# New cost numbers for an order of work that is laid out ahead, and later loads of the memory rows, in an encoder layer

## The chip, the cores and the metric

The kernel runs on one core of a Trainium2 chip. The metric is the device time of one execution in microseconds (us). Three runs of the kernel before gave a median of 1152.73 us (1152.61 to 1153.55). Five engines are spoken of: TensorE (PE in the profile; its weight loads are PEld), VectorE (DVE), ScalarE (ACT), GpSimd (POOL) and SyncE (SP), which issues most of the loads.

## The reference

One encoder layer for a sequence of 256 tokens of width 2048, in float32. Cut to what matters:

```python
# h = rms_norm(x); one combined input projection
x = x + W_out @ concat(mla(h), diff_attention(h))    # 8 MLA heads, 4 difference heads
x = x + cross_attention(rms_norm(x), rms_norm(mem))  # 4 heads into 256 memory tokens
x = x + swiglu(rms_norm(x))                          # hidden width 5632
return rms_norm(x)

def rms_norm(x, g, eps=1e-6):
    return x * rsqrt(mean(x * x, axis=-1) + eps) * g
```

The MLA half projects the normed rows to a query latent of 512, a key and value latent of 256 and a rotary key of 64, norms the latents and projects them up; rotary tables (sine and cosine of position times frequency) are computed from the positions. The memory has 256 rows of 2048.

## The kernel before

Weights are streamed from memory once. Each weight tile (wraw, up to 1 MB) is split into a high part wh, a cast on ScalarE, and a low part wl, the remainder, a subtraction on VectorE. Activations are split in the same way (names ending in _h and _l). A product is then three matmuls: high by high, high by low, low by high (mm in the listing). The rows on which a wide product rests are handled in pairs of k-tiles. A plain pair takes the three matmuls for each quarter of the result. A pair of kind W takes seven products of sums in place of eight ones, so it needs sums and forms of the activations (sums, forms_h, forms_l) and of the weights (tsum) from VectorE and ScalarE. The string DN_KINDS says which pairs of the down projection are of which kind.

The stages, in time order by the profile: the latent product (6 to 48 us: 16 k-tiles of x0T against w_in_lat, 512 columns into acc and 320 into acckv), the wide input projection and the MLA heads (from 48 us), the difference heads, the output product (wide_add over w_out), the product of the memory with w_xk, the cross-attention, and from about 470 us on the feed-forward layer, whose hidden chunks alternate with groups of the down projection (wide_add over w_dn). In the list called groups each entry gives the chunks computed before it and the order in which its pairs are then taken.

Nothing of this is issued in the order of the code. Each call on an engine is recorded by Plan.record as an Op with three modelled numbers from Plan.cost: how long the engine is busy, how long until the result is usable (lag), and how long a transfer takes. Plan.emit makes a list schedule: first one run that takes operations as they come ready, then two rounds in which each operation has a wanted time, found backwards from the modelled starts of TensorE's work. In Plan.run every engine has a time at which it is free, transfers share one queue, and of the operations that could start soon the one wanted first is taken. The order that comes out is the program order of each engine. Real waits are semaphores, put in for data and for buffers that are handed on; so a wrong number in the model never makes a wrong result, only an order in which an engine stands behind something that is late. op.after(other, False) adds a rule for the order alone and puts in no semaphore. All recorded operations carry the line of record's inner function, L224, so the profile is read by tile names.

Four parts of the code are spoken of.

- Squares of the memory rows. The rows (tiles mn, four of 512 KB from in_mem, buffers of the pool act, which has 24) are loaded by GpSimd and squared with a running sum by ScalarE (junk<-mn, eight operations, sums in mss); VectorE adds them up and GpSimd takes the power (rstdm), and VectorE scales the product with w_xk by it (xk). rstdm is not needed before that.
- The first k-tile. Its weight tile is loaded and cast in two pieces of 512 and 320 columns (cut=QL); VectorE makes x0T_h from xraw and gains.
- The rope tables. GpSimd computes them (ang, a1r, turns, prod) from posi, which SP loads behind the first seven k-tiles. Its queue also holds the powers rstd (for the norm of x), rq and rkv (for the latents). VectorE's cq<-acc,rstd and ckv<-acckv,rstd scale the latents; TensorE transposes them (pt<-ident,ckv).
- The group changes of the down projection. res are the sums of a finished hidden chunk; TensorE transposes them (pt<-ident,res), ScalarE copies them back and makes hT_h, VectorE makes hT_l; W pairs use forms_h and forms_l of the same data.

Of the kernel before, what the change touches and what calls it, by code (L numbers as in the profile page):

```python
# [18 lines left out]
P = 128  # L19
# [159 lines left out]
class Plan:  # L179


    HANDOVER, CHOICE = 0.06, 0.3

    def __init__(self, tc):
# [31 lines left out]
    def record(self, engine, method, args, kw):  # L216
        out = [x for x in (kw.get("out", args[0] if args else None), kw.get("accum_out")) if isinstance(x, Ref)]
        ins = [x for x in list(args) + list(kw.values()) if isinstance(x, Ref) and not any(x is o for o in out)]
        busy, lag, transfer = self.cost(engine, method, out, ins, kw, args)

# [8 lines left out]
        for ref, writes in [(r, True) for r in out] + [(r, False) for r in ins]:  # L229
            t, mask = ref.tile, ref.mask()  # L230
# [12 lines left out]

    def cost(self, engine, method, out, ins, kw, args):
        if method == "dma_start":
            size = max(x.cols() for x in out + ins) * 512
            return 0.86 if engine == "gpsimd" else 0.06, 2.0 + size / 375e3, size / 381e3
        n = max([x.cols() for x in out[:1]] + ([x.cols() for x in ins[:1]] if "reduce" in method else []))
        if engine == "tensor":
            if method == "transpose":  # L250
                return 0.108, 0.33, 0.0
            return 0.0134 + n / 2400, 0.2134 + n / 2400, 0.0
        if engine == "gpsimd":
            t = 0.15 + n * 0.0045
            return t, t + 0.1, 0.0
        if engine == "vector":
            if n <= 16 and "reduce" not in method:
                t = 0.07
            elif method == "scalar_tensor_tensor":
                t = 0.127 + n * 1.05e-3  # L260
            elif method in ("tensor_scalar", "memset"):
                t = 0.03 + n / 1024
            else:
                t = 0.068 + n / 960
            return t, t + 0.082, 0.0
        t = 0.044 + 0.855e-3 * n if ins and ins[0].tile.whole else 0.092 + 0.842e-3 * n
        if isinstance(kw.get("scale"), Ref):
            t += 0.09
        if kw.get("accum_out") is not None:
            t += 0.093  # L270
        return t, t + (0.2 if kw.get("accum_out") is not None else 0.1), 0.0

# [8 lines left out]
    def run(self, chain, wanted, emit):  # L281
# [11 lines left out]
        for engine in ("sync", "scalar"):  # L293
            in_turn([o for o in self.ops if o.engine == engine and o.transfer])
        open_ops, free, queue, picks, starts, ended = {}, {}, 0.0, {}, {}, 0.0
        emitted, to_go, slots = [], {}, {}
# [24 lines left out]
        for _ in self.order:  # L321
# [20 lines left out]
            if o.transfer:  # L342
                begun = max(start, queue)
                queue, end = begun + o.transfer, begun + o.lag
            starts[o] = start
# [93 lines left out]
def encoder_block(tc: tile.TileContext, a, out):  # L439
# [736 lines left out]
    for tt in range(NT):  # L1176
        n = nat("xk")
# [279 lines left out]
```

## Time and profile before

| what | value |
|---|---|
| median of three runs | 1152.73 us (1152.61 to 1153.55) |
| the profiled execution | 1153.09 us |
| its span in the trace | 1151.2 us |
| TensorE busy | 1132.5 us, 98% of the span |
| VectorE busy | 1017.4 us, 88% |
| ScalarE busy | 695.4 us, 60% |
| GpSimd busy | 54.8 us, 5% |
| read from memory | 219.11 MB |

The span is from the first to the last instruction that the trace shows; 1.9 us of the execution lie outside. Busy time of TensorE is read from pipelined matmuls: one of 512 columns shows 0.39 us, but the next one starts about 0.23 us after it. A number in brackets behind a row of the timeline is the idle time of that engine before the instruction, and what ended it. In tables by stage, the columns are the stretch, its length, and the busy time and number of instructions of each engine, TensorE's granted clock, the share of the DMA engines' time and the rate in GB/s.

### The profile page before, as it was taken

Reading aid. Unit: us, or ns where it says so; the run is one execution under the profiler, and the core shown is the slowest. Engines: PE = TensorE matmul, PEld = TensorE weight load, DVE = VectorE, ACT = ScalarE, POOL = GpSimd, SP = SyncE. Lnnn points to the kernel's source line nnn. Section 1 sums busy time; section 2 is a strip of 40 time slices with the busy share of each in tenths; the row PEclk is TensorE's granted clock in tenths of the full one; section 3 lists DMA queues with packets and bytes.
Section 4 is the critical chain, followed back from the end, with each engine's and each line's share of the span. In section 5 each row is a group of like instructions: output and inputs, shape, how many; then the busy total and the mean of one; then the engine's idle time right before and its main releaser. Section 6 shows DMA issues by size and latency. Waiting matters only on the chain.

```text
span 1151.2 us, 14663 instructions
## 1 busy us (share of the span) xinstructions
PE 1132.5 (98%) x5360; PEld 941.0 (82%) x5360; DVE 1017.4 (88%) x1378; ACT 695.4 (60%) x999; POOL 54.8 (5%) x75
## 2 busy tenths in 40 slices
PE   8999999999999999999999999999999999999997
PEld 6889888888888788887878888888788888888786
DVE  4788768778988767799999999999999999999995
ACT  6757445466765545656665565666665565756762
POOL 4920000000000000000000000000000000000000
PEclk9999999999999999999999999999999999999999
DMA  9734354456554444555545556565455565556453
GB/s 353 292 135 170 110 183 145 150 180 228 193 209 179 147 178 158 184 179 198 213 172 216 210 194 216 183 219 200 169 217 212 190 219 183 201 208 250 153 200 122
DMA packets 35496, 222.16 MB, mean 193 GB/s; under 512 B 4320, under 2 KB 5600, under 8 KB 11104
## 3 DMA queue, kind: packets, MB, share of 16 engines
q1 hardware_dynamic: 33696, 216.60, 52.6%
q0 software_dynamic: 864, 3.15, 0.8%
q10 hardware_dynamic: 864, 1.47, 0.4%
q8 instruction: 42, 0.69, 0.2%
q14 instruction: 30, 0.25, 0.1%
HBM read 219.11 MB, written 2.10 MB: 192 GB/s over the span
## 4 chain that ended last, share of the span: by engine, by line
PE 81%; DVE 10%; POOL 4%; ACT 2%; issue 2%; DMA 1%; SPq 0%; POOLq 0%; DVEq 0%; ACTq 0%
PE acc L224 63%; PE q L224 13%; DVE wl L224 3%; PE pt L224 2%; POOL prod L224 1%; DVE res L224 1%; PE qT L224 1%; DMA wraw<-in_w_in_lat 1%; POOL ang L224 1%; DVE tsum L224 1%; POOL turns L224 1%; DVE nm L224 1%; PE psc L224 1%; DVE sums L224 1%; DVE forms_l L224 1%
## 5 line engine op out<-in xcount | busy, mean ns | idle before, releaser
L224 DVE TENSOR_TENSOR wl<-wraw,wh 128x1024 fp32r<-128x1024 f32 (+2 forms) x401 | 449.2, 1133 | 92.2 <-ACT wh L224 90.7
L224 ACT CAST wh<-wraw 128x1024 fp32r<-128x1024 f32 (+2 forms) x401 | 388.0, 978 | 234.7 <-PE acc L224 192.3
L224 ACT CAST wh<-tsum 128x1024 fp32r<-128x1024 f32 (+1 forms) x118 | 119.5, 1017 | 127.4 <-DVE tsum L224 73.7
L224 DVE TENSOR_TENSOR wl<-tsum,wh 128x1024 fp32r<-128x1024 f32 (+1 forms) x118 | 137.9, 1174 | 5.8 <-PE acc L224 4.0
L224 PE MATMUL acc<-wh,x2n_h 128*128 128x512 f32 x320 | 124.7, 390 | 0.0
L224 PE MATMUL acc<-wh,x2n_l 128*128 128x512 f32 x320 | 124.6, 389 | 0.0
L224 PE MATMUL q<-wh,forms_h 128*128 128x512 f32 x231 | 91.4, 396 | 1.4 <-ACT res L224 1.4
L224 PE MATMUL q<-wh,forms_l 128*128 128x512 f32 x231 | 90.0, 390 | 0.0
L224 PE MATMUL acc<-wl,x0T_h 128*128 128x512 f32 x224 | 89.2, 398 | 0.6 <-DVE wl L224 0.6
L224 PE MATMUL acc<-wh,x0T_h 128*128 128x512 f32 x224 | 89.0, 397 | 0.6 <-DVE x0T_h L224 0.6
L224 PE MATMUL acc<-wh,x0T_l 128*128 128x512 f32 x224 | 88.6, 395 | 0.0
L224 PE MATMUL acc<-wl,x2n_h 128*128 128x512 f32 x320 | 86.1, 390 | 0.0
L224 PE MATMUL q<-wl,forms_h 128*128 128x512 f32 x231 | 81.0, 392 | 1.1 <-DVE wl L224 1.1
L224 DVE TENSOR_TENSOR tsum<-tsum,wraw 128x512 f32<-128x512 f32 x118 | 80.7, 684 | 0.8
L224 PE MATMUL acc<-wh,forms_l 128*128 128x512 f32 x192 | 74.9, 390 | 0.0
L224 PE MATMUL acc<-wh,forms_h 128*128 128x512 f32 x192 | 74.9, 390 | 0.0
L224 DVE TENSOR_TENSOR tsum<-wraw 128x1024 f32<-128x1024 f32 (+1 forms) x64 | 72.2, 1134 | 1.5 <-DMA wraw<-in_w_out 1.5
L224 PE MATMUL acc<-wh,hT_h 128*128 128x512 f32 x188 | 73.4, 390 | 0.0
L224 PE MATMUL acc<-wh,hT_l 128*128 128x512 f32 x188 | 73.2, 389 | 0.0
L224 PE MATMUL acc<-wl,forms_h 128*128 128x512 f32 x192 | 72.9, 390 | 0.0
L224 PEld LDWEIGHTS acc<-wh,x2n_l 128*128 128x128 f32 x320 | 60.1, 188 | 12.5
L224 PEld LDWEIGHTS acc<-wh,x2n_h 128*128 128x128 f32 x320 | 60.1, 188 | 12.5
(377 smaller groups left out, 2149.7 us busy)
## 6 DMA issues: line engine op xcount, KB each, us to landing
wraw<-in_w_gate SPq DMA_DIRECT2D x44, 1024.0 KB, 4.8
wraw<-in_w_up SPq DMA_DIRECT2D x44, 1024.0 KB, 4.8
wraw<-in_w_dn SPq DMA_DIRECT2D x41, 1024.0 KB, 4.8
wraw<-in_w_in SPq DMA_DIRECT2D x24, 1024.0 KB, 4.8
wraw<-in_w_out SPq DMA_DIRECT2D x16, 1024.0 KB, 4.9
wraw<-in_w_in_lat SPq DMA_DIRECT2D x5, 832.0 KB, 6.2
wraw<-in_w_xk SPq DMA_DIRECT2D x4, 1024.0 KB, 5.5
wraw<-in_w_xq SPq DMA_DIRECT2D x4, 1024.0 KB, 4.8
```

Source lines behind the costliest of these rows:

```text
L224: getattr(getattr(self.tc.nc, engine), method)(*[made(x) for x in args], **{k: made(x) for k, x in kw.items()})
```

## The change

It has three parts.

- Costs. Plan.cost gets other numbers: issuing a load takes 0.55 us on GpSimd and 0.45 us on SP and ScalarE (before 0.86 and 0.06); arithmetic on GpSimd takes 0.59, 0.7 or 1.0 us by its columns (before 0.15 + 0.0045 for each); VectorE's scalings are priced by whether they read PSUM; an activation with a bias tile costs as one with a scale tile; lags of TensorE and ScalarE are shorter. Plan.run starts each engine at a time of its own (BEGUN), lets small transfers pass the queue, and adds 0.9 us to loads started in the first 5 us.
- Memory rows. Each of their four loads is placed in the order after the last weight split of the output product (load.after(mixed, False)). This is a rule of the order; no semaphore is added.
- Groups two and three of the down projection take pair 4 before pair 2.

```diff
+    BEGUN = {"tensor": 0.6, "vector": 0.8, "scalar": 0.7, "sync": 0.7, "gpsimd": 0.3}
...
         if method == "dma_start":
             size = max(x.cols() for x in out + ins) * 512
-            return 0.86 if engine == "gpsimd" else 0.06, 2.0 + size / 375e3, size / 381e3
+            return {"gpsimd": 0.55, "sync": 0.45, "scalar": 0.45}[engine], 2.0 + size / 375e3, size / 381e3
         n = max([x.cols() for x in out[:1]] + ([x.cols() for x in ins[:1]] if "reduce" in method else []))
+        in_psum = bool(ins) and ins[0].tile.whole
         if engine == "tensor":
-            if method == "transpose":
-                return 0.108, 0.33, 0.0
-            return 0.0134 + n / 2400, 0.2134 + n / 2400, 0.0
+            t = 0.108 if method == "transpose" else 0.0134 + n / 2400
+            return t, t + 0.14, 0.0
         if engine == "gpsimd":
-            t = 0.15 + n * 0.0045
-            return t, t + 0.1, 0.0
+            if method in ("memset", "affine_select", "tensor_copy"):
+                t = 0.1 + n * 1.2e-3
+            else:
+                t = 0.59 if n == 1 else 0.7 if n == 2 else 1.0
+            return t, t + 0.03, 0.0
         if engine == "vector":
             if n <= 16 and "reduce" not in method:
-                t = 0.07
+                t = 0.08
             elif method == "scalar_tensor_tensor":
                 t = 0.127 + n * 1.05e-3
-            elif method in ("tensor_scalar", "memset"):
-                t = 0.03 + n / 1024
+            elif method == "tensor_scalar":
+                t = 0.129 + n * 1.035e-3 if in_psum else n / 960
+            elif method == "tensor_tensor_reduce":
+                t = 0.145 + n / 960
+            elif method == "tensor_copy":
+                t = n / 960
             else:
                 t = 0.068 + n / 960
             return t, t + 0.082, 0.0
-        t = 0.044 + 0.855e-3 * n if ins and ins[0].tile.whole else 0.092 + 0.842e-3 * n
-        if isinstance(kw.get("scale"), Ref):
-            t += 0.09
+        t = 0.044 + 0.855e-3 * n if in_psum else 0.092 + 0.842e-3 * n
+        if isinstance(kw.get("scale"), Ref) or isinstance(kw.get("bias"), Ref):
+            t += 0.09 if n < 512 else 0.15
         if kw.get("accum_out") is not None:
             t += 0.093
-        return t, t + (0.2 if kw.get("accum_out") is not None else 0.1), 0.0
+        return t, t + (0.15 if kw.get("accum_out") is not None else 0.08), 0.0
...
-        open_ops, free, queue, picks, starts, ended = {}, {}, 0.0, {}, {}, 0.0
+        open_ops, free, queue, picks, starts, ended = {}, dict(self.BEGUN), 0.0, {}, {}, 0.0
...
             if o.transfer:
-                begun = max(start, queue)
-                queue, end = begun + o.transfer, begun + o.lag
+                begun = max(start, queue) if o.transfer > 0.15 else start
+                queue, end = max(queue, begun + o.transfer), begun + o.lag + (0.9 if start < 5.0 else 0.0)
...
+    mixed = last_split[0]
...
-            nc.gpsimd.dma_start(out=mn, in_=a["mem"][tt * P:(tt + 1) * P, c * 1024:(c + 1) * 1024])
+            load = nc.gpsimd.dma_start(out=mn, in_=a["mem"][tt * P:(tt + 1) * P, c * 1024:(c + 1) * 1024])
+            load.after(mixed, False)
...
-    groups = [([0], (0, 1, 4, 2, 5, 3)), ([1, 2], (0, 1, 2, 4, 5, 3, 7, 6)), ([3, 4], (0, 1, 2, 4, 5, 3, 7, 6))]
+    groups = [([0], (0, 1, 4, 2, 5, 3)), ([1, 2], (0, 1, 4, 2, 5, 3, 7, 6)), ([3, 4], (0, 1, 4, 2, 5, 3, 7, 6))]
```

SP's loads keep their order. Three places show how the others move. The recorded line is L224 before and L225 after.

**ScalarE, the first k-tiles.** Before, behind its two loads of the first weight tile:

```order
L224 CAST wh<-wraw 128x512
L224 ACTIVATE junk,mss<-mn 128x512
L224 CAST wh<-wraw 128x320
L224 ACTIVATE x0T_h<-xraw,gains 128x256
L224 ACTIVATE junk,mss<-mn 128x512
```

After:

```order
L225 CAST wh<-wraw 128x512
L225 CAST wh<-wraw 128x320
L225 ACTIVATE x0T_h<-xraw,gains 128x256
L225 CAST wh<-wraw 128x512
L225 CAST wh<-wraw 128x320
```

The squares of the memory rows left this place (six more stood a little later in it); all eight now stand among the casts of the product with w_xk. On GpSimd the four loads of mn went from the head of the queue to behind the four powers rd of the difference heads, ahead of x1Tr and rstdm.

**VectorE, end of the latent product.** The splits of 1024 columns are of the first weights of the wide input projection, which follows. Before:

```order
L224 TENSOR_TENSOR wl<-wraw,wh 128x1024 x6
L224 TENSOR_SCALAR cq<-acc,rstd_539 128x512 x2
L224 TENSOR_SCALAR ckv<-acckv,rstd_539 128x320
L224 TENSOR_SCALAR rq<-ss 128x1
L224 TENSOR_SCALAR ckv<-acckv,rstd_539 128x320
```

After:

```order
L225 TENSOR_TENSOR wl<-wraw,wh 128x1024 x4
L225 TENSOR_SCALAR cq<-acc,rstd_496 128x512 x2
L225 TENSOR_TENSOR wl<-wraw,wh 128x1024
L225 TENSOR_SCALAR ckv<-acckv,rstd_496 128x320
L225 TENSOR_SCALAR rq<-ss 128x1 x2
L225 TENSOR_SCALAR ckv<-acckv,rstd_496 128x320
```

The scalings of the latents, which need GpSimd's rstd, moved ahead of the fifth and the sixth of those splits.

**VectorE, the first changed group of the down projection.** Here res_7258 (after: res_7259) and res_7287 are the newly finished hidden chunk, of which hT is made, and res_6561 and res_6585 the one of which forms are made. Before:

```order
L224 TENSOR_TENSOR forms_l<-res_6561,forms_h 128x256
L224 TENSOR_TENSOR wl_7453<-tsum,wh_7434 128x1024
L224 TENSOR_TENSOR sums<-res_6561,res_6585 128x128
L224 TENSOR_TENSOR sums<-res_6561,sums 128x128
L224 TENSOR_TENSOR forms_l<-res_6585,forms_h 128x256 x2
L224 TENSOR_TENSOR wl<-wraw,wh 128x1024
L224 TENSOR_TENSOR hT_l<-res_7258,hT_h 128x4x128
L224 TENSOR_TENSOR hT_l<-res_7287,hT_h 128x4x128
```

After:

```order
L225 TENSOR_TENSOR forms_l<-res_6585,forms_h 128x256 x2
L225 TENSOR_TENSOR wl<-wraw,wh 128x1024 x2
L225 TENSOR_TENSOR tsum<-wraw 128x1024
L225 TENSOR_TENSOR forms_l<-sums,forms_h 128x512
L225 TENSOR_TENSOR hT_l<-res_7259,hT_h 128x4x128
L225 TENSOR_TENSOR wl<-wraw,wh 128x1024
L225 TENSOR_TENSOR hT_l<-res_7287,hT_h 128x4x128
```

Here the split of the summed weight (wl_7453 before) went behind hT_l, and each hT_l stands just ahead of a split for the plain pair that uses it. On TensorE the matmuls of that plain pair come 24 matmuls earlier than before, ahead of those of the W pair.

More of the change, by code (lines that the diff above doesn't have):

```diff
@@ L218, in record @@
         ins = [x for x in list(args) + list(kw.values()) if isinstance(x, Ref) and not any(x is o for o in out)]
-        busy, lag, transfer = self.cost(engine, method, out, ins, kw, args)
+        busy, lag, transfer = self.cost(engine, method, out, ins, kw)
         def fn():
@@ L242, in record, with cost @@
         return op
-    def cost(self, engine, method, out, ins, kw, args):
+    def cost(self, engine, method, out, ins, kw):
         if method == "dma_start":
             size = max(x.cols() for x in out + ins) * 512
-            return 0.86 if engine == "gpsimd" else 0.06, 2.0 + size / 375e3, size / 381e3
+            return {"gpsimd": 0.55, "sync": 0.45, "scalar": 0.45}[engine], 2.0 + size / 375e3, size / 381e3
         n = max([x.cols() for x in out[:1]] + ([x.cols() for x in ins[:1]] if "reduce" in method else []))
+        in_psum = bool(ins) and ins[0].tile.whole
         if engine == "tensor":
-            if method == "transpose":
-                return 0.108, 0.33, 0.0
-            return 0.0134 + n / 2400, 0.2134 + n / 2400, 0.0
+            t = 0.108 if method == "transpose" else 0.0134 + n / 2400
+            return t, t + 0.14, 0.0
         if engine == "gpsimd":
-            t = 0.15 + n * 0.0045
-            return t, t + 0.1, 0.0
+            if method in ("memset", "affine_select", "tensor_copy"):
[3 more added lines that the diff above has]
+            return t, t + 0.03, 0.0
         if engine == "vector":
             if n <= 16 and "reduce" not in method:
-                t = 0.07
+                t = 0.08
             elif method == "scalar_tensor_tensor":
                 t = 0.127 + n * 1.05e-3
-            elif method in ("tensor_scalar", "memset"):
-                t = 0.03 + n / 1024
+            elif method == "tensor_scalar":
[4 more added lines that the diff above has]
+                t = n / 960
             else:
```

## The prediction

> **What bounds the kernel now.** I read the page's engine shares and strips first, then the releasers of idle time, then busy time by stage, then the timeline of the first 20 us.
>
> ```profile
> span 1151.2 us, 14663 instructions
> PE 1132.5 (98%) x5360; PEld 941.0 (82%) x5360; DVE 1017.4 (88%) x1378; ACT 695.4 (60%) x999; POOL 54.8 (5%) x75
> PE   8999999999999999999999999999999999999997
> ```
>
> TensorE is the bound: it idles only 18.7 us in the span (1151.2 − 1132.5), and an edit that removes no matmul can win only that idle time, plus time in which matmuls run slower than they could. The stages:
>
> ```profile
> core 0: us, PE busy (x) PEld busy (x) DVE busy (x) ACT busy (x) POOL busy (x), PEclk, DMA share, GB/s
> 6.00:15.30 9.30, 7.67 (x24) 5.76 (x24) 2.88 (x7) 4.52 (x11) 0.00 (x0) 1.00 1.03 400
> 15.30:28.20 12.90, 12.22 (x62) 10.08 (x62) 9.13 (x14) 12.40 (x26) 8.05 (x11) 1.00 1.03 401
> 28.20:48.40 20.20, 20.20 (x109) 17.81 (x109) 17.04 (x21) 16.24 (x32) 18.70 (x19) 1.00 0.86 323
> 48.40:64.80 16.40, 16.40 (x75) 13.51 (x74) 11.61 (x27) 11.01 (x23) 15.68 (x20) 1.00 0.50 186
> 64.80:69.50 4.70, 3.80 (x25) 3.15 (x24) 4.28 (x7) 2.81 (x5) 0.95 (x2) 1.00 0.29 112
> 104.00:135.00 31.00, 30.35 (x214) 27.41 (x213) 27.85 (x68) 18.48 (x49) 0.00 (x0) 1.00 0.17 60
> 170.00:190.00 20.00, 19.47 (x116) 16.46 (x115) 17.12 (x42) 13.28 (x39) 1.42 (x2) 1.00 0.35 127
> 250.00:260.00 10.00, 9.47 (x57) 7.76 (x56) 7.23 (x16) 7.75 (x19) 1.38 (x2) 1.00 0.32 107
> 340.00:367.00 27.00, 27.00 (x141) 22.74 (x140) 25.53 (x35) 17.00 (x26) 0.69 (x1) 1.00 0.54 191
> 385.00:400.00 15.00, 13.79 (x83) 11.56 (x82) 13.69 (x30) 9.36 (x24) 0.00 (x0) 1.00 0.36 135
> 810.00:826.00 16.00, 15.31 (x75) 12.27 (x74) 15.96 (x26) 11.58 (x19) 0.00 (x0) 1.00 0.26 84
> 1060.00:1076.00 16.00, 15.30 (x75) 12.28 (x73) 15.96 (x26) 11.51 (x19) 0.00 (x0) 1.00 0.27 101
> ```
>
> The third row is the latent product running freely: 109 matmuls in 20.2 us, 0.1853 us each, TensorE never idle. The same kind of matmul fills the first two rows: 86 of them take 22.2 us where that pace gives 15.9. So 6.3 us are lost before 28.2 us, more than in any later place. In those two rows the transfers are full (share 1.03). In the last two, VectorE is (15.96 of 16), so an order that is wrong there has no slack to hide in.
>
> **The start, part by part.** Why it is slow:
>
> ```profile
> 1.23 2.29 POOL L224 DMA_DIRECT2D mn<-in_mem  x4 [0.80 <-POOLq L1446]
> 4.24 0.62 ACT L224 CAST wh<-wraw 128x512 fp32r<-128x512 f32 x1 [1.11 <-DMA wraw<-in_w_in_lat]
> 4.89 0.69 DVE L224 TENSOR_TENSOR wl<-wraw,wh 128x512 fp32r<-128x512 f32 x1 [3.77 <-ACT wh L224]
> 5.99 0.76 PE L224 MATMUL acc<-wh,x0T_h 128*128 128x512 f32 x1 [0.58 <-DVE x0T_h L224]
> 7.69 0.63 ACT L224 ACTIVATE junk<-mn 128x512 bf16<-128x512 f32 x1 [2.83 <-DMA mn<-in_mem]
> 8.81 0.63 PE L224 MATMUL acckv<-wh,x0T_h 128*128 128x320 f32 x1 [1.63 <-ACT wh L224]
> 10.81 0.98 ACT L224 CAST wh<-wraw 128x512 fp32r<-128x512 f32 x2 [1.03 <-DMA wraw<-in_w_in_lat]
> 12.97 0.60 PE L224 MATMUL acc<-wl,x0T_h 128*128 128x512 f32 x1
> 13.40 0.41 PE L224 MATMUL acc<-wh,x0T_l 128*128 128x512 f32 x1
> q0 software_dynamic: 546, 2.03, 71.5%
> q1 hardware_dynamic: 492, 0.89, 29.1%
> q1 hardware_dynamic: 2119, 5.57, 103.9%
> ```
>
> (The queue rows: q0 carries the memory rows, q1 the weights; the first two are of 4 to 12 us, the last of 13 to 27 us.) Three things are visible. ScalarE, in order, sits 2.83 us behind a memory row before it may cast the 320 columns of the first weight, and TensorE waits 1.63 us for that. The memory rows take 2.03 of 2.92 MB in 4 to 12 us, so the weights get 0.89 MB in 8 us (111 GB/s) where they get 5.57 MB in 14 us (398 GB/s) once alone; the second weight is castable only at 10.81. And matmuls go every 0.43 us until 13.4 (12.97 to 13.40), about twice the later step.
>
> The change removes all three causes. ScalarE's queue begins with both casts of the first weight and no square of a memory row. The SP loads are in the same order, now without a rival queue. VectorE makes the first x0T_h ahead of wl, so the first matmul needs only the cast that ends at 4.86: I take 5.1 (5.0 to 6.0). Then 195 matmuls (24 + 62 + 109) by 0.1853 are 36.1 us. To this I add what the slow pace costs. Measured from the first real matmul it lasted 7.2 us before, with two gaps in it (5.99 to about 13.2); that again would cost half of it, 3.6. If the 11 warming matmuls already serve, 0. There are now no gaps, so I take nearer to nothing: 1.2. The end of the stage goes from 48.4 to 5.1 + 36.1 + 1.2 = 42.4: **−6.0** (−3.6 to −7.3). A cross-check: 2.03 MB at 398 GB/s is 5.1 us of transfer taken out of a stretch whose transfers were full.
>
> The Trainium skill (TensorE: Matmul & The Clock Gate, Part 1: The HAM clock gate) says that the full clock is granted after one fully busy window of about 3.4 us of a free-running raster. By that, unbroken work from 1.18 us would be at full clock between 4.6 and 8.0, which makes the term 0 to 1.5 in place of 1.2; this trace, which has gaps, only agrees that a broken start stays slow.
>
> Behind the start come two later waits. GpSimd makes the rope tables, alone, from the landing of the positions on:
>
> ```profile
> 19.37 0.18 POOL L224 CAST posf<-posi 128x2 f32<-128x2 int32 x1 [14.89 <-DMA posi<-in_pos]
> L224 POOL TENSOR_TENSOR turns<-turns,prod x8: 599/685/1264, 24.4 to 51.5; 128x192 f32<-128x192 f32 x8
> 54.90 0.73 POOL L224 TENSOR_TENSOR rstd<-rstd,mhalf 128x2 f32<-128x2 f32 x1
> 63.81 1.29 POOL L224 TENSOR_TENSOR rkv<-rkv,mhalf 128x1 f32<-128x1 f32 x1
> 67.39 0.44 PE L224 MATMUL pt<-ident,ckv 128*128 128x128 f32 x2 [0.90 <-DVE gT L224]
> ```
>
> The positions stand behind 3.14 MB on SP; at about 390 KB/us from 4 us on, with half of a megabyte landed by then, they arrive near 13.6 (an estimate). The chain from posf to rstd is 35.5 us, one 0.7 us operation shorter in the new order, but its first third now meets a busier VectorE. The 28.2 to 48.4 row has 19 operations in 20.2 us, 1.06 each; 27 of them by 42.4, then 9 by 0.7 to 1.06, end rstd at 48.7 to 51.9. In the changed VectorE order the two products cq<-acc,rstd stand before the fifth of the wide weights that follow the latent weights, so TensorE now depends on that rstd: the six weights of 48.4 to 64.8 take 2.73 us each, so the fifth is wanted at 53.3; less one split and two cq (about 2.5) rstd must be there by 50.8. The middle of the estimate holds that: 0, with 1 us on TensorE for each us that it is late (up to 1.1). rkv no longer has sind and rstdm ahead of it, and its whole chain is earlier by about as much as TensorE is; of the 0.9 us idle in 64.8 to 69.5 I take half: **−0.5** (−0.9 to +1.1).
>
> **The memory rows themselves.**
>
> ```profile
> gfb<-in_g_final POOLq DMA_DIRECT2D x2, 512.0 KB, 7.3
> L224 DVE TENSOR_SCALAR xk<-acc,rstdm x2: 740/742/743, 362.6 to 363.2; 128x512 f32<-128x512 f32 x2
> ```
>
> Their loads now stand on GpSimd's queue behind the fourth rd of the difference heads; behind them are x1Tr and rstdm. Each still has to get a free one of the 24 act buffers, which the work ahead of them in the order frees between about 256 and 310 us of before's time, while the squares stand where 342 to 356 were and xk uses rstdm at 362.6. GpSimd's other pair of loads of this size took 7.3 us to land, late in the program, so they are there some 25 us early. Eight squares of 0.63 (the 7.69 row) are 5.0 us more for ScalarE in 340 to 367, where it idles 10.0 of 27 and TensorE waits for nothing: **0**. If that cover were gone, up to 5.0.
>
> **Other moves.** The new costs reorder TensorE in the attention heads, the difference heads and the cross softmax, in the windows of 104 to 135, 170 to 190, 250 to 260 and 385 to 400. Idle there: 0.65 + 0.53 + 0.53 + 1.21 = 2.9. A new order can win all of it or lose; no row shows it. Taking 40%: **−1.2** (−2.9 to +1.4, the same share spent elsewhere).
>
> **The two groups of the down projection.** The plain pair now precedes the W pair; its hT is asked for 24 matmuls earlier, 5.5 us at 0.23 (the spacing of 512-column matmuls, 811.01 to 811.24).
>
> ```profile
> 811.01 0.39 PE L224 MATMUL acc<-wh,hT_l 128*128 128x512 f32 x1
> 811.24 1.07 PE L224 MATMUL acc<-wl,hT_h 128*128 128x512 f32 x4
> 815.79 0.49 PE L224 MATMUL q<-wh,forms_h 128*128 128x512 f32 x1
> 821.18 0.50 PE L224 MATMUL q<-wh,forms_h 128*128 128x512 f32 x1 [0.69 <-ACT res L224]
> 821.37 1.28 DVE L224 TENSOR_TENSOR hT_l<-res,hT_h 128x512 fp32r<-128x512 f32 x2
> ```
>
> Where the new hT is wanted (at 815.79 of before) it was ready only at 822.65 (821.37 + 1.28); but ScalarE and VectorE had put casts and splits for the other pair before it, and the new orders on both put hT first. I take half of the 0.69 idle at each of the two places as won: **−0.7** for both (−1.4, to +11.0 if hT stays where it was).
>
> **Sum.** −6.0 − 0.5 + 0 − 1.2 − 0.7 = −8.4. The profiled execution took 1153.09, 0.36 above the median of 1152.73; 1153.09 − 8.4 = 1144.7, and by the median 1144.3. Forecast 1144.5. Its own bounds, without the far ends, are about 1141 to 1148.
>
> **Rivals.**
>
> *Half a start.* The weights stay near 111 GB/s for some other reason, or the clock steps up as late as before. Then only ScalarE's block (1.63) and the earlier first matmul (0.9) go, and a half of the rest: about −3.5, 1149.2. For it: only one row shows the weights' queue alone, and that later. Against it: the 28.2 row needs only 323 GB/s for the full pace, and 398 was had. Chance 0.17.
>
> *GpSimd becomes the bound* of 40 to 65 us. If the 36 operations take the 1.26 of the slow end of their row, rstd ends at 13.6 + 36 by 1.35 = 62.2, 11.4 after 50.8, and the whole start is lost: −8.4 + 11.4 = +3.0, 1156. It decides against the change from a mean near 1.27 us an operation on. Against it: the mean of before, under a VectorE 84% busy, is 1.06. The Trainium skill (SBUF — State Buffer, SBUF: two separate sides) says that VectorE and GpSimd lock one pair of ports against each other for whole instructions; the row's spread from 0.60 to 1.26 agrees. Chance 0.06; half of it as probable to cost only some us (1148).
>
> *The plain pair comes too early.* VectorE is full at 810 to 826 (15.96 of 16), and hT cannot come earlier than before: 2 by 5.5 lost, no 0.7 won, so −7.7 + 11.0 = +3.3, 1156.4: slower than before. It decides from 3.9 us late at each place on. For it: VectorE never idles there. Against it: what stands before hT_l in VectorE's old order is work for the pair that now comes later. Chance 0.06.
>
> *The loads don't wait for the output product.* The order is only one of the plan, and the waits that issue them are the buffers'. That is so, I think, but costs nothing; it gives the forecast.
>
> *All idle goes:* −7.3 − 0.9 − 2.9 − 1.4 = −12.5, 1140.6. Chance 0.06.
>
> **How the numbers follow.** Forecast 0.62, half a start 0.17, GpSimd 0.09 with its milder form, plain pair 0.06, all idle 0.06. A difference under 0.2% (2.3 us) can't be told from no change here. Faster by more: 0.62 + 0.17 + 0.06 + 0.04 = 0.89; same 0.05; slower 0.06. The range 1140.8 to 1150.0 holds the forecast, all of half a start, and nearly all idle gone.
>
> **What would show it.** Right: the first real matmul near 5.1, the second weight cast by 8, posf near 13.6, matmuls at 0.23 by 8, the first wide weight's matmul at 42 to 43, no idle TensorE at 52 to 55 that VectorE's wl releases, squares of memory rows at 335 to 350 with no wait on a DMA, and under 0.7 us idle in the two group changes. Wrong: weights under 300 GB/s in 4 to 12 us, TensorE released by VectorE's wl for several us near 53, or by hT at the group changes.

## The result: 1146.28 us, and the profile after

The changed kernel takes 1146.28 us (median of 4 runs, 1145.23 to 1146.49) against 1152.74 for the kernel before: a ratio of 0.9941, with an interval of 0.9923 to 0.9958. It wins 6.5 us where 8.2 were forecast. Its profiled execution took 1146.09, 7.0 under that of before. One execution of all that follow, 1902.66 us in the run with the old groups, had a granted clock of 0.56 and is left out of that run's median.

The page of the changed kernel: the shares, and TensorE's strip.

```profile
span 1144.3 us, 14653 instructions
PE 1128.8 (99%) x5360; PEld 938.8 (82%) x5360; DVE 1016.5 (89%) x1378; ACT 695.1 (61%) x999; POOL 57.7 (5%) x75
PE   9999999999999999999999999999999999999997
```

TensorE is busy 3.7 us less, with the same 5360 matmuls, since fewer of them run at the slow pace at the start (the first 95 matmuls are busy for 20.4 us in place of 24.3); its idle time falls from 18.7 to 15.5. Where the time went is best seen by number: the n-th matmul is of the same stage in both kernels, so the difference of its start in the two traces, read at the ends of stages, gives what each stage won or lost.

| stage | won (−) or lost (+), us | predicted |
|---|---|---|
| to the first real matmul | −0.9 | −0.9 |
| to the end of the latent product, with the line above | −6.7 | −6.0 |
| wide projection and transposes of the latents | +1.0 | −0.5 |
| MLA heads | −1.2 | |
| difference heads | −0.1 | |
| output product, product with w_xk and cross-attention | −1.1 | |
| the last three together | −2.4 | −1.2 |
| feed-forward, to matmul 5100, with the two group changes | +0.5 | −0.7 |
| the last group | +0.7 | 0 |
| sum | −6.9 | −8.4 |

The start, from the timeline of the changed kernel:

```profile
4.31 1.03 ACT L225 CAST wh<-wraw 128x512 fp32r<-128x512 f32 x2 [1.18 <-DMA wraw<-in_w_in_lat]
4.58 0.35 DVE L225 TENSOR_SCALAR x0T_h<-xraw,gains 128x256 fp32r<-128x256 f32 x1 [3.46 <-DMA gains<-in_gains]
5.08 0.85 PE L225 MATMUL acc<-wh,x0T_h 128*128 128x512 f32 x2
7.17 0.98 ACT L225 CAST wh<-wraw 128x512 fp32r<-128x512 f32 x2 [1.39 <-DMA wraw<-in_w_in_lat]
8.71 0.39 PE L225 MATMUL acc<-wl,x0T_h 128*128 128x512 f32 x1
8.94 0.39 PE L225 MATMUL acc<-wh,x0T_l 128*128 128x512 f32 x1
14.01 0.18 POOL L225 CAST posf<-posi 128x2 f32<-128x2 int32 x1 [12.33 <-DMA posi<-in_pos]
```

The row of the table by stages (length, then busy time and number on PE, PEld, DVE, ACT, POOL, granted clock, DMA share, GB/s), and then the weights' queue from 4 to 12 us (packets, MB, share of the time of the transfers):

```profile
5.00:41.70 36.70, 36.59 (x194) 32.04 (x193) 28.64 (x39) 28.02 (x51) 25.52 (x28) 1.00 0.97 368
```

```profile
q1 hardware_dynamic: 1470, 2.84, 99.5%
```

The weights now have 2.84 MB of 4 to 12 us (355 GB/s) where they had 0.89. Both casts of the first weight follow each other, the second weight is cast at 7.17 in place of 10.81, and 194 matmuls fill 36.7 us with 0.1 idle. The step from the slow to the full pace came with the second real matmul.

The next row is where time was lost, with what stands before it on GpSimd and VectorE:

```profile
47.95 0.72 POOL L225 TENSOR_TENSOR rstd<-rstd,mhalf 128x2 f32<-128x2 f32 x1
56.58 1.23 POOL L225 TENSOR_SCALAR cosd<-cosd,rstd 128x128 f32<-128x128 f32 x1 [1.17 <-ACT cosd L225]
57.79 0.56 POOL L225 TENSOR_TENSOR rkv<-rkv,mhalf 128x1 f32<-128x1 f32 x1
58.39 0.35 DVE L225 TENSOR_SCALAR ckv<-ckv,rkv 128x256 f32<-128x256 f32 x1 [1.05 <-POOL rkv L225]
58.66 2.44 DVE L225 TENSOR_TENSOR wl<-wraw,wh 128x1024 fp32r<-128x1024 f32 x2
61.02 1.27 DVE L225 TENSOR_TENSOR gT<-pt,gains 128x512 f32<-128x512 f32 x2
61.76 0.44 PE L225 MATMUL pt<-ident,ckv 128*128 128x128 f32 x2 [1.93 <-DVE gT L225]
```

The second rkv stands in GpSimd's queue behind cosd, which waits 1.17 for ScalarE's cosine and then takes 1.23. So VectorE waits 1.05 for it at ckv, makes two splits, and only then gT, for which TensorE stands 1.93 us (0.90 before). In the kernel before, VectorE had one split there:

```profile
65.14 0.47 DVE L224 TENSOR_SCALAR ckv<-ckv,rkv 128x256 f32<-128x256 f32 x1 [0.46 <-POOL rkv L224]
65.52 1.21 DVE L224 TENSOR_TENSOR wl<-wraw,wh 128x1024 fp32r<-128x1024 f32 x1
66.66 1.27 DVE L224 TENSOR_TENSOR gT<-pt,gains 128x512 f32<-128x512 f32 x2
```

Set side by side, the second rkv ends 6.75 us earlier than before (58.35 for 65.10) and ckv starts 6.75 earlier, just about as much as TensorE gained (6.7). But gT starts only 5.64 earlier, since two splits (2.36 us from their start to gT) stand in the place of one (1.14). The loss of 1.0 against the kernel before is the second split; the rkv that stands behind cosd is why nothing was won there.

The memory rows, later, in GpSimd's timeline and then as ScalarE's group (count, durations, first and last start):

```profile
250.96 0.79 POOL L225 DMA_DIRECT2D mn<-in_mem  x1
267.51 0.55 POOL L225 DMA_DIRECT2D mn<-in_mem  x1 [15.76 <-ACT mT_h L225]
300.14 0.54 POOL L225 DMA_DIRECT2D mn<-in_mem  x1 [32.08 <-PE acc L225]
301.05 0.54 POOL L225 DMA_DIRECT2D mn<-in_mem  x1 [0.37 <-PE acc L225]
```

```profile
L225 ACT ACTIVATE junk<-mn x8: 622/625/631, 335.3 to 348.1; 128x512 bf16<-128x512 f32 x8
```

They don't wait for the output product, which ends near 337: the releasers are the users of the buffers. The last is issued at 301, 34 us before the first square, and ScalarE waits for none of them.

### The profile page after: what moved, and what is told of

Same layout as the page of the kernel before. It is cut to its first block, busy times and chain, and to the rows that moved or that the text cites. A ratio compares the mean times of both kernels' runs of the same rounds, so it can differ in the third digit from the quotient of the medians.

```text
span 1144.3 us, 14653 instructions
## 1 busy us (share of the span) xinstructions
PE 1128.8 (99%) x5360; PEld 938.8 (82%) x5360; DVE 1016.5 (89%) x1378; ACT 695.1 (61%) x999; POOL 57.7 (5%) x75
## 4 chain that ended last, share of the span: by engine, by line
PE 80%; DVE 10%; POOL 3%; issue 2%; DMA 2%; ACT 2%; SPq 0%; POOLq 0%; DVEq 0%; ACTq 0%
PE acc L225 62%; PE q L225 13%; DVE wl L225 4%; PE pt L225 2%; PE psc L225 1%; DVE tsum L225 1%; POOL prod L225 1%; PE qT L225 1%; POOL ang L225 1%; DVE res L225 1%; POOL turns L225 1%; DVE forms_l L225 1%; PE po L225 1%; DMA wraw<-in_w_dn 1%; DVE nm L225 1%
## 5 line engine op out<-in xcount | busy, mean ns | idle before, releaser
L225 ACT CAST wh<-wraw 128x1024 fp32r<-128x1024 f32 (+2 forms) x401 | 387.3, 977 | 224.8 <-PE acc L225 178.5
L225 DVE TENSOR_TENSOR wl<-wraw,wh 128x1024 fp32r<-128x1024 f32 (+2 forms) x401 | 447.7, 1130 | 83.1 <-ACT wh L225 82.0
L225 ACT CAST wh<-tsum 128x1024 fp32r<-128x1024 f32 (+1 forms) x118 | 119.6, 1017 | 127.2 <-DVE tsum L225 77.0
L225 DVE TENSOR_TENSOR wl<-tsum,wh 128x1024 fp32r<-128x1024 f32 (+1 forms) x118 | 138.1, 1174 | 7.7 <-PE acc L225 4.3
L225 PE MATMUL acc<-wh,x2n_h 128*128 128x512 f32 x320 | 124.6, 389 | 0.0
L225 PE MATMUL acc<-wh,x2n_l 128*128 128x512 f32 x320 | 124.6, 389 | 0.0
L225 PE MATMUL q<-wh,forms_h 128*128 128x512 f32 x231 | 91.2, 395 | 0.0
L225 PE MATMUL q<-wh,forms_l 128*128 128x512 f32 x231 | 90.0, 390 | 0.0
L225 PE MATMUL acc<-wh,x0T_h 128*128 128x512 f32 x224 | 88.2, 395 | 0.1
L225 PE MATMUL acc<-wl,x0T_h 128*128 128x512 f32 x224 | 88.1, 394 | 0.0
L225 PE MATMUL acc<-wh,x0T_l 128*128 128x512 f32 x224 | 87.8, 393 | 0.0
L225 PE MATMUL acc<-wl,x2n_h 128*128 128x512 f32 x320 | 86.1, 390 | 0.0
L225 PE MATMUL q<-wl,forms_h 128*128 128x512 f32 x231 | 81.0, 392 | 1.2 <-DVE wl L225 1.2
L225 DVE TENSOR_TENSOR tsum<-tsum,wraw 128x512 f32<-128x512 f32 x118 | 80.8, 684 | 0.8
L225 PE MATMUL acc<-wh,hT_l 128*128 128x512 f32 x188 | 73.8, 393 | 1.2 <-DVE hT_l L225 1.1
L225 PE MATMUL acc<-wh,forms_l 128*128 128x512 f32 x192 | 74.9, 390 | 0.0
L225 PE MATMUL acc<-wh,forms_h 128*128 128x512 f32 x192 | 74.9, 390 | 0.0
L225 DVE TENSOR_TENSOR tsum<-wraw 128x1024 f32<-128x1024 f32 (+1 forms) x64 | 72.3, 1135 | 1.9 <-DMA wraw<-in_w_out 1.0
L225 PE MATMUL acc<-wh,hT_h 128*128 128x512 f32 x188 | 73.4, 390 | 0.0
L225 PE MATMUL acc<-wl,forms_h 128*128 128x512 f32 x192 | 73.0, 390 | 0.0
L225 PEld LDWEIGHTS acc<-wh,x2n_l 128*128 128x128 f32 x320 | 60.1, 188 | 12.5
L225 PEld LDWEIGHTS acc<-wh,x2n_h 128*128 128x128 f32 x320 | 60.1, 188 | 12.4
```

The costliest lines, as they stand in the source:

```text
L225: getattr(getattr(self.tc.nc, engine), method)(*[made(x) for x in args], **{k: made(x) for k, x in kw.items()})
```

## The experiments

For each run the same table by stages was made; the numbers are differences of the matmuls' starts from the kernel before, in the profiled execution of each.

| kernel | to the end of the latent product | transposes of the latents | heads and cross-attention | feed-forward | median of the runs |
|---|---|---|---|---|---|
| the change | −6.7 | +1.0 | −2.4 | +1.2 | 1146.3 |
| rows only | −5.5 | +2.7 | +0.1 | +0.1 | 1149.8 |
| costs only | +3.3 | −0.9 | −2.3 | +1.1 | 1153.4 |
| old groups | −6.6 | +2.6 | −2.5 | +1.1 | 1146.1 (three runs) |
| rows loaded twice | −1.3 | +1.0 | −2.4 | +1.3 | 1152.0 |
| two rows twice | −3.7 | +1.8 | −2.4 | +1.2 | 1150.0 (one run) |
| rkv first | −6.5 | −1.1 | −2.4 | +1.2 | 1144.7 |
| rstd later | −7.1 | +6.7 | −2.4 | +1.3 | 1150.8 |
| positions early | −5.9 | −1.1 | −2.4 | +1.3 | 1144.9 |
| rkv first, dearer power | −6.1 | −0.2 | −3.8 | +1.3 | 1144.0 |
| old costs, rkv first | −6.3 | +0.4 | 0.0 | 0.0 | 1147.7 |
| the change again | −7.0 | +1.0 | −2.5 | +1.2 | 1146.1 |

### The memory rows alone

```diff
 (kernel before)
+            load.after(mixed, False)
```

> The kernel before with one thing changed: the loads of the four memory rows are ordered behind the last split of the output product. Old costs, old groups. Theory A (the memory rows make the slow start, by their transfers and by ScalarE standing behind them): the latent product ends at 42 to 44 us in place of 48.3, nearly all of the 6.7 us that the changed kernel wins by then, and the time is 1146.5 to 1148.5. The first real matmul stays near 6.0, since VectorE still makes wl first. Theory C (the new costs make the start): the latent product ends at 47 to 48.4, time 1151 to 1153.

The ratio is 0.9971 (0.9960 to 0.9981): 1149.82 us, 1.3 above the range of theory A. The start did as theory A says: 5.5 us by the end of the latent product, with the first real matmul at 6.02. What this expectation missed is the place behind it, where 2.7 were lost: 2.14 us of idle time before the transposes of ckv and a granted clock of 0.50 behind it. Theory C is out as far as the start goes.

### The costs alone

```diff
 (changed kernel)
-            load.after(mixed, False)
-    groups = [([0], (0, 1, 4, 2, 5, 3)), ([1, 2], (0, 1, 4, 2, 5, 3, 7, 6)), ([3, 4], (0, 1, 4, 2, 5, 3, 7, 6))]
+    groups = [([0], (0, 1, 4, 2, 5, 3)), ([1, 2], (0, 1, 2, 4, 5, 3, 7, 6)), ([3, 4], (0, 1, 2, 4, 5, 3, 7, 6))]
```

> The changed kernel without the rule for the memory rows and with the old groups: the new costs alone. The planner then loads the rows at the start and puts the first square ahead of ScalarE's very first cast and six more among the next casts. Theory A: nothing is won at the start, the latent product ends at 48 to 53 us; the later moves win about 2, time 1150 to 1156. Theory C: the latent product ends before 45, time 1146 to 1149.

1153.43 us, a ratio of 1.0005 (0.9995 to 1.0014): no change. The timeline shows the plan's mistake:

```profile
7.58 0.63 ACT L225 ACTIVATE junk<-mn 128x512 bf16<-128x512 f32 x1 [4.45 <-DMA mn<-in_mem]
8.21 0.60 ACT L225 CAST wh<-wraw 128x512 fp32r<-128x512 f32 x1
8.86 1.22 PE L225 MATMUL acc<-wh,x0T_h 128*128 128x512 f32 x2 [3.45 <-ACT wh L225]
```

ScalarE stands 4.45 us before its first cast, for a square that nobody needs before 350 us. So the new numbers lose 3.3 at the start if the rows are free to be loaded there; they win 0.9 at the transposes and 2.3 in the heads and the cross-attention, and give back 1.1 in the feed-forward part.

### The old groups

> The changed kernel with the old pair order in groups two and three. By the prediction's step (0.35 us won at each of the two places): 0.7 slower than the changed kernel, 1147.0. By the changed kernel's trace, where TensorE idles there as long as before, for hT_l in place of a copy on ScalarE: the same within 0.5, 1145.8 to 1146.8. If the plain pair came too early it would be faster by over 1.

The edit is the second line pair of the diff above alone. The median is 1146.12 (1145.40 to 1147.61), next to 1146.28 of the changed kernel. In the two group changes the order of the pairs makes no difference that the traces show (feed-forward +1.1 against +1.2). It trades one wait for another: with the old order TensorE waits 0.70 in the group change for ScalarE's res, with the new one 0.55 for VectorE's hT_l. The changed kernel, by stage and in the timeline:

```profile
802.00:818.00 16.00, 15.39 (x75) 12.12 (x74) 16.00 (x24) 10.41 (x15) 0.00 (x0) 1.00 0.43 158
```

```profile
808.12 1.22 DVE L225 TENSOR_TENSOR wl<-wraw,wh 128x1024 fp32r<-128x1024 f32 x1
809.25 0.68 DVE L225 TENSOR_TENSOR hT_l<-res,hT_h 128x512 fp32r<-128x512 f32 x1
809.99 0.50 PE L225 MATMUL acc<-wh,hT_l 128*128 128x512 f32 x1 [0.55 <-DVE hT_l L225]
```

VectorE is busy 16.00 of 16; whatever is asked for earlier there comes out of it at the expense of the next thing.

What sets this run's profile apart from the changed kernel's, up to 800 us the same program, is 1.6 us behind the idle time at 62 us. The stages of this run, and then of the changed kernel:

```profile
59.00:62.00 3.00, 1.07 (x9) 0.76 (x8) 3.00 (x4) 0.63 (x2) 3.00 (x3) 1.00 0.29 101
62.00:65.20 3.20, 3.20 (x11) 2.53 (x11) 3.11 (x6) 1.65 (x4) 0.20 (x1) 0.51 0.17 69
```

```profile
59.00:62.00 3.00, 1.07 (x10) 0.75 (x8) 3.00 (x4) 0.63 (x2) 3.00 (x3) 1.00 0.31 82
62.00:65.20 3.20, 3.20 (x17) 2.64 (x16) 3.11 (x6) 1.66 (x5) 0.15 (x1) 1.00 0.21 87
```

The same 1.9 us of idle time; after it the granted clock is 0.51 in the one (11 matmuls in 3.2 us) and 1.00 in the other (17).

### The memory rows loaded a second time

```diff
 (changed kernel)
+    mem_loads = []
+    for tt in range(2):
+        for c in range(2):
+            spare = act.tile([P, 1024], F32, name="spare", tag="act")
+            o = nc.gpsimd.dma_start(out=spare, in_=a["mem"][tt * P:(tt + 1) * P, c * 1024:(c + 1) * 1024])
+            o.busy, o.lag, o.transfer = 0.0, 14.0, 0.0
+            mem_loads.append(o)
-    nc.gpsimd.memset(mhalf, -0.5)
+    halves = nc.gpsimd.memset(mhalf, -0.5)
+    for o in mem_loads:
+        halves.after(o, False)
```

> The changed kernel, with the four loads of the memory rows issued a second time at the head of GpSimd's queue, into spare buffers that nothing reads (2.1 MB more to move; the squares and their own loads stay late). It puts back the shared transfers and not ScalarE's wait. Theory A: transfers are the larger part; weights get 110 to 150 GB/s from 4 to 12 us, posf comes near 19, the latent product ends at 45.5 to 47.5 in place of 41.7, time 1150 to 1152. Theory B (ScalarE's wait is all of it): it ends at 41.5 to 42.5, time 1146 to 1147.

1151.98 us. The queues of 4 to 12 us, and two rows of the timeline:

```profile
q0 software_dynamic: 536, 1.99, 69.8%
q1 hardware_dynamic: 520, 0.92, 30.4%
```

```profile
10.49 0.98 ACT L225 CAST wh<-wraw 128x512 fp32r<-128x512 f32 x2 [2.10 <-DMA wraw<-in_w_in_lat]
11.16 1.22 PE L225 MATMUL acc<-wh,x0T_h 128*128 128x512 f32 x2 [3.40 <-ACT wh L225]
```

The weights are back at 115 GB/s, the second one comes at 10.49, and 5.4 of the 6.7 us are gone again, though ScalarE never stands behind a memory row here. Theory B is out: ScalarE's wait and the order of the first matmul are left with 1.3 at most. (That is a remainder: no run has their share alone, and two profiles of the changed kernel differ by 0.3 at this place.)

### Two of the four rows a second time

The same edit with `for tt in range(1)`.

> As the run with the memory rows loaded twice, but with two of the four extra loads (1 MB). That run's latent product ended at 47.0 us against 41.6. If the loss goes by the bytes that are moved ahead of the weights, half of it is left: an end at 44.0 to 44.8. If it is the presence of a second queue, or a clock that falls back once TensorE stands: 45.5 to 47.

The latent product ended at 44.7, 2.9 later than in the changed kernel, against 5.4 for four rows: the loss goes by the bytes, 1 MB for 2.7 to 2.9 us. The casts of the fifth weight, for which ScalarE waits in all three kernels, show the same: 11.82 in the changed kernel, 14.42 with two rows, 16.78 with four. In the run with four rows the granted clock also fell to 0.50 from 10.9 to 14.3 us, behind the 3.40 us of idle time; there the third weight, castable only at 13.95, sets the pace and not the clock.

### rkv before cosd and sind

```diff
 (changed kernel, latents_normalized)
-        for t in (cosd, sind):
-            for tt in range(NT):
-                nc.gpsimd.tensor_scalar(out=t[:, tt], in0=t[:, tt], scalar1=rstd1[:, tt:tt + 1], ...)
         for tt in range(NT):
             rms_rows(ckvs[tt], acc_kv[tt], tt, KVL + DR, KVL, "rkv")
+        for t in (cosd, sind):
+            for tt in range(NT):
+                nc.gpsimd.tensor_scalar(...).after(powed[0], False)    # the second power rkv
```

> The changed kernel with the four scalings cosd and sind ordered on GpSimd behind the second power rkv. Theory D (the idle TensorE at 59 to 62 us of the changed kernel is VectorE's ckv waiting for that power, which stands behind cosd, which waits for ScalarE's cosine): ckv comes about 1.5 earlier, the two idle us shrink to 0.5 to 1, time 1144.6 to 1145.4. Theory E (VectorE's two splits ahead of gT set it): the idle stays at about 2, time 1146 to 1146.6.

1144.74 us, a ratio of 0.9929 (0.9914 to 0.9943). Theory D, and more of it than expected: the idle time is gone, as GpSimd's timeline and the row of the stage show.

```profile
54.91 0.55 POOL L225 TENSOR_TENSOR rkv<-rkv,mhalf 128x1 f32<-128x1 f32 x1 [0.29 <-DVE rkv L225]
56.62 1.72 POOL L225 TENSOR_SCALAR cosd<-cosd,rstd 128x128 f32<-128x128 f32 x1
```

```profile
56.00:63.00 7.00, 7.00 (x40) 5.89 (x39) 6.91 (x10) 4.39 (x7) 4.80 (x5) 1.00 0.31 119
```

rkv comes at 54.91 in place of 57.79, and TensorE is busy 7.00 of 7, though VectorE still makes two splits between ckv and gT (2.45 us). So theory E, that those splits alone set the wait, is out; an order with one split there was not tried.

### rstd later

```diff
 (changed kernel)
     less_whole(turns, turns)
+    spare, late = tp.tile([P, NT, NF], F32, name="spare"), []
+    for n in range(4):
+        late.append(nc.gpsimd.tensor_scalar(out=spare, in0=turns, scalar1=0.25, scalar2=None, op0=ALU.mult))
+        late[-1].busy = late[-1].lag = 0.0
...
     rstd1 = rstd_of(xs1, EPS, "rstd1")
+    for o in late:
+        plan.ops[-1].after(o, False)
```

> The changed kernel with four more operations on GpSimd ahead of the power rstd, which nothing reads. By the prediction's coupling (VectorE's scalings cq stand ahead of the split that TensorE needs, and are released by rstd): rstd comes 4 to 6 us later, near 53; the fifth split had about 1.3 us of room in the changed kernel, so TensorE stands 3 to 5 us at 52 to 56 us, and the time is 1149 to 1152. If VectorE makes it up or the coupling isn't one: 1146 to 1147.

1150.79 us.

```profile
47.69 3.02 POOL L225 TENSOR_SCALAR spare<-turns 128x192 f32<-128x192 f32 x4
50.68 0.73 POOL L225 TENSOR_TENSOR rstd<-rstd,mhalf 128x2 f32<-128x2 f32 x1
54.04 0.50 PE L225 MATMUL acc<-wl,x0T_h 128*128 128x512 f32 x1 [1.38 <-DVE wl L225]
64.48 0.69 PE L225 MATMUL pt<-ident,ckv 128*128 128x128 f32 x2 [3.36 <-DVE gT L225]
```

The four operations took 3.0 us together, less than expected, and rstd came 2.7 later where 4 to 6 were expected. The coupling is real: TensorE, which never waited for that split in the changed kernel, now does, for 1.38 (3 to 5 were expected). It waits again at the transposes of ckv, for 3.36, and the slow clock follows that. In all 2.7 us on GpSimd cost 4.5 in the medians.

### The positions early

```diff
 (changed kernel)
-        if i == 3:
+        if i == 1:
             nc.sync.dma_start(out=posi, in_=a["pos"])
```

> The changed kernel with the loads of posi and invf put behind the first xraw and weight loads on SP's queue, ahead of the k-tiles of the second to seventh weights. GpSimd's chain then begins near 8 to 9 us in place of 14. Theory D: its end, and with it rkv, comes 4 to 5 us earlier, the idle at the transposes of ckv falls to under 1, time 1144.5 to 1145.5; the first weights come 0.1 later. Theory E: no change, 1146 to 1146.6.

1144.94 us, a ratio of 0.9931 (0.9916 to 0.9945), and no idle time at the transposes either. The positions landed at 6.73, rstd ended at 41.8, and the second rkv at 49.6, 8.8 earlier than in the changed kernel where 4 to 5 were expected. Two edits that share the earlier rkv remove the same wait. (With these start times the planner also put rkv ahead of cosd by itself, so the run does not tell the early start from the order.)

### A dearer power of two columns

```diff
 (run with rkv first)
-                t = 0.59 if n == 1 else 0.7 if n == 2 else 1.0
+                t = 0.59 if n == 1 else 1.7 if n == 2 else 1.0
```

> The run with rkv first, with one number more: GpSimd's operations of two columns (the powers rstd and rd) cost 1.7 us in the plan in place of 0.7. In the changed kernel they took 1.62 and 0.70 in the difference heads, and TensorE stood 0.88 us at 176.9 before a transposition pdt of what the 1.62 one releases. If that price put pdt too early, the 0.88 goes and the time is 1143.6 to 1144.2 against 1144.7 of the run with rkv first; if VectorE's own load there sets it, no change (1144.4 to 1145.0).

1144.04 us (1143.32 to 1144.20), a ratio of 0.9922 (0.9907 to 0.9937), the best of all, though its interval overlaps that of the run with rkv first. The wait at pdt (0.88 us by the spacing of the matmuls, 0.72 idle in the trace) is gone, and another 0.36 idle in the second pair of difference heads; in exchange this profiled execution had 0.67 idle at the transposes of ckv. In the changed kernel those powers took from 0.69 to 1.71 us:

```profile
L225 POOL TENSOR_TENSOR rd<-rd,mhalf x4: 692/1160/1710, 175.8 to 249.3; 128x2 f32<-128x2 f32 x4
```

### Old costs with the rows late and rkv first

The edits of the memory rows alone and of rkv first, made in the kernel before.

> The kernel before, with the loads of the memory rows after the output product and the second power rkv ahead of cosd and sind; old costs and old groups, so what the new cost numbers bring is left out. The run with the rows alone won 5.5 us by the end of the latent product and then lost 2.7 at the transposes of ckv (2.4 idle, and a slow clock behind it). If rkv behind cosd was the cause of that, the loss turns into a gain of about 1: 1146.0 to 1147.2, so the new costs are worth 1.5 to 2.5 us of the run with rkv first. If the old order loses there for another reason: 1148.5 to 1150.

1147.65 us (ratio 0.9958, 0.9943 to 0.9973), half a us above the range. The 2.7 lost at the transposes shrink to 0.4 where a gain of about 1 was expected; 1.36 of idle time are left; the second rkv took 1.46 us here and ended only at 59.3. By the medians the new costs are worth 2.9 us of the run with rkv first, above the 1.5 to 2.5 that were expected. By the profiles it is 3.0: 1.5 at the transposes, 2.4 in the heads and the cross-attention, 0.2 at the start, less 1.2 in the feed-forward part.

### The changed kernel again

> The changed kernel once more. Its four times fell at 1145.2 and at 1146.1 to 1146.5, and the run with the old groups, the same up to 800 us, showed a slow clock of about 3.3 us behind the idle time at 61 us (1.6 us lost) where the first profile of the changed kernel showed none. If the idle time of about 2 us sometimes brings the clock down and sometimes not, these times fall in two groups some 1.3 to 1.6 apart, while those of the two kernels with rkv first stay within 1.

The runs gave 1145.47, 1145.74, 1146.51 and 1147.70; this profile has the same 1.93 us idle at the transposes and no slow clock behind them. The eight times of the two batches do not fall in two clean groups, and the kernels with rkv first, which were to stay within 1, spread over 1.6 (rkv first), 0.9 (dearer power) and 2.2 (old costs). That a slow clock sometimes follows the idle time is shown by the profiles above; that it makes the whole spread of the times is not.

## Why the prediction was right or wrong, step by step

- **The start, −6.0 forecast, −6.7 found.** Right in size, and for its reasons. First real matmul: 5.1 forecast, 5.08. Of the 1.2 us for the slow pace 0.2 came: the full pace was there with the second real matmul. The Trainium skill (TensorE: Matmul & The Clock Gate, Part 1) would have the step between 4.6 and 8.0, and it came at 5.5. In four other executions, with the same warming matmuls from 1.17 or 1.18 us on, it came at 3.9 to 4.1 (old groups, rows loaded twice, rkv first, dearer power), earlier than that rule allows, so here the moment differs by over 1 us between executions. Of the causes, the shared transfers are worth 5.4, as the run with the rows loaded twice shows; the cross-check with 2.03 MB had given 5.1. The rival of half a start is out.
- **The transposes of the latents, −0.5 forecast, +1.0 found.** This step failed. It took half of the 0.9 us of idle time as won, because rkv no longer has sind and rstdm ahead of it. That is so, but it has cosd ahead, as before, and cosd now waits for ScalarE's cosine; so rkv came as much earlier as TensorE did, 6.75 us, and no more. The step looked at what left GpSimd's queue and not at what stayed, nor at what that waits for. And it did not look at VectorE's order behind ckv, where a second split now stands ahead of gT and makes it 1.0 us late. The runs show the first part: with rkv ahead of cosd the stage wins 1.1, with both splits still there. The second is read from the two timelines.
- **rstd and the fifth split, 0 forecast, 0 found.** rstd was there at 48.7, the early end of the range of 48.7 to 51.9. In the run with rstd later it ended at 51.4 and cost 1.4 at the split, so it is wanted by about 50.0; the step had 50.8, for a latent product that ends 0.6 later than it did. The GpSimd rival was right in kind, but its chain did not slow down as a whole: 33.9 us from the start of posf to that of rstd, 35.5 before. Two numbers of this working don't follow from what it states. 3.14 MB less half of one at 390 KB/us from 4 us on gives 10.8 us for the positions, not 13.6; posf started at 14.01, so that number was near by luck. And the rival's end at 62.2 takes 1.35 us an operation; with the 1.26 that it names it is 59, which only uses up the gain.
- **The memory rows themselves, 0.** Right: between the difference heads and the cross softmax, where the squares now stand, the difference of the two kernels changes by 0.15, to the better, and the loads went by their buffers from 251 us on, as that rival said, at no cost.
- **Other moves, −1.2 forecast, −2.4 found**, within the bounds. The first number was a share of the idle time for want of a row, so its size was a guess. The cross softmax won 1.0 of its 1.21 us. The MLA heads won 1.2, more than the 0.65 idle in their window: by the spacing of the matmuls the three waits there were 1.1 long, as a matmul of 512 columns shows 0.39 us busy for a step of 0.23, so idle time read from busy time comes out short. The difference heads lost the 1.06 that they had and got 1.13 elsewhere, 0.72 of it at pdt behind the power rd, which the dearer price took away.
- **The two groups, −0.7 forecast, +0.1 or nothing found.** Wrong by its size: half of the 0.69 at each place was taken as won, and it came back as a wait of 0.55 for hT_l. The +0.5 of this stage is not of the groups: it is +0.4 with the old order too, and with the costs alone. The rival that the plain pair comes too early did not happen either: the new orders on ScalarE and VectorE brought hT_l forward by 4.7 to 5.8 us at each place, for the 5.5 us that were needed.
- **The last group, 0 forecast, +0.7 found.** Not in the sum at all. It is there in all runs with the new costs, whatever the groups, and in none with the old ones. In the trace they are small gaps of 0.1 to 0.25 before matmuls with wl and forms, and VectorE works there without a break. Which of the new numbers does it was not tried.
- **The sum, −8.4 forecast, −6.9 found.** The start and the other moves came out 1.9 us better than forecast, the transposes, the feed-forward part and the last group 3.4 worse. That the time lies only 1.8 us from the forecast is in part luck, as these errors cancel.

## What to carry to other kernels

A transfer that nobody needs for 300 us can be the dearest thing in the first ten: look at which queue has the bytes while the first weights are awaited, and price the start by bytes (here 1 MB was 2.7 to 2.9 us). Where a list of work waits in order, read what is still ahead of the awaited operation, not only what was moved away, and what that waits for in turn, on every engine of the chain up to TensorE. And a table of costs that is nearer to the measured ones does not by itself give a better order: alone it gave none here, since what it decided wrongly at the start cost as much as it won later.

## What the runs showed that was not expected

- Idle time of about 2 us can cost twice. Behind the wait at the transposes the granted clock was 0.50 for 3.4 us after 2.14 us of idle time (rows only), for 3.4 after 1.93 (old groups) and for 6.8 after 3.36 (rstd later); it stayed at 1.00 after 1.93 in three others (the change twice, rows loaded twice) and after 2.72 (two rows twice). At the start, 3.40 us of idle time brought it down to 0.50 too (rows loaded twice), and 2.45 did not (two rows twice). The Trainium skill (TensorE: Matmul & The Clock Gate, Part 1) gives an idle window of about 3.4 us as the condition; here 1.93 was enough in one execution and 2.72 was not in another.
- The granted clock of the profile reads 1.00 over the first 13 us of the kernel before, where matmuls of 512 columns go every 0.43 us, half the later pace (0.23). At the start the pace has to be read from the spacing of the matmuls, not from that column.
- GpSimd's loads and SP's loads do not share evenly: with both at work from 4 to 12 us the first took 70% of the transfer time and the second 30%, in the kernel before and again when the rows were loaded twice.
- GpSimd's operations vary within one execution of the changed kernel: arithmetic on 128x192 numbers took from 0.60 to 1.63 us, and a power of 128x2 numbers from 0.69 to 1.71.
